# First loads of a two-layer decoder trunk cut into K tiles and interleaved, with constant products on TensorE at the start

## The chip, the cores and the metric

The kernel runs on one core of a Trainium2 chip. The metric is the device time of one execution in microseconds (us), the median over runs. One launch computes the whole reference.

## The reference

Two decoder layers over 256 positions of width 2048, all in float32. What matters here is the start of layer 0:

```python
def _rmsnorm(x, g):
    x32 = x.astype(jnp.float32)
    y = x32 * lax.rsqrt(jnp.mean(x32 * x32, axis=-1, keepdims=True) + EPS)
    return (y * g.astype(jnp.float32)).astype(x.dtype)

for l in range(DEPTH):                       # DEPTH = 2
    h = _rmsnorm(x, attn_norm_g[l])          # x: (1, 256, 2048)
    proj = h @ w_in[l]                       # w_in[l]: (2048, 6144)
    q, k, v, gate_b, gate_c, conv_in = jnp.split(proj, splits, axis=-1)
    # differential attention on q, k, v; gated causal convolution on the rest
    ...
    x = x + jnp.concatenate([attn, conv], axis=-1) @ w_out[l]
    hm = _rmsnorm(x, mlp_norm_g[l]) @ w_up[l]
    x = x + jnp.square(jax.nn.relu(hm)) @ w_down[l]
```

## The kernel before

**Products in three terms.** Every large product runs on TensorE in the type float32r. To keep accuracy, both operands are split into a rounded part (`hi`, made by a ScalarE copy) and the remainder (`lo`, made by a VectorE subtraction), and three of the four products are summed: hi x hi, hi x lo, lo x hi (`TERMS`). So for each K tile (128 rows of the contraction) and each of the two tiles of 128 positions, `linear` issues three matmuls of 512 columns (line 338): six per K tile, and sixteen K tiles for one block of 512 output columns. The first block is the first half of q of layer 0.

**The activations.** x lies in four tiles `xs[n]` of 512 columns, each four K tiles. `Norm.chunk` (line 394) takes one: for each of two pairs j of K tiles it transposes them on TensorE into a PSUM bank (line 402), and evicts each with the gain multiplied in, as a rounded part on ScalarE (line 248) and a remainder on VectorE (line 249). Then it squares the two position tiles of x on ScalarE for the norm's sum (line 412). The row factors of the norm are applied after the product, so matmuls need not wait for them. `Parts.ready` says that a chunk is there.

**The weights.** `Weights` holds a list of jobs. A job loads 512 KB (two K tiles by 512 columns) on SyncE's DMA queue (line 298), and `halves` splits it into `hi` (line 282) and `lo` (line 283). In layer 0 the first two jobs are split in two pieces, one K tile each. `take` makes jobs up to three ahead of the one that is used. Loads use four buffers, and `hi` and `lo` three each. `load_early` issues loads ahead of their jobs: `first_loads` (line 986) alternates two weight loads and one chunk of x.

**The order of the work.** TensorE's instructions run in the order in which the program is written. For the other engines and the DMA queues a scheduler, at build time, chooses the order by its own model of the times, with the order written as the priority; on the chip each engine then executes that fixed order. `late` (line 118) ties an instruction behind the one that was written just ahead of it on the same engine. `Background` holds generators that are advanced by ticks: `linear` ticks once after each K tile, and in a loop while it waits for a chunk of x. So the wait numbers decide behind which K tile a chunk's transposes stand: chunk 0 in front of K tile 0, chunk 1 behind K tile 1, chunk 2 behind K tile 5.

Of the kernel before, what the change touches and what calls it, by code (L numbers as in the profile page):

```python
# [15 lines left out]
P = 128  # L16
# [85 lines left out]
def trunk(ctx: ExitStack, tc: tile.TileContext, x, w_in, w_out, conv_w, q_norm_g, k_norm_g,  # L102
# [19 lines left out]
    def bank(name):  # L122
        return ps.tile([P, CH], F32, tag="bank", name=name)
# [8 lines left out]

    def load_x(n, cuts=1):
        for c in range(cuts):
            lo, hi = c * CH // cuts, (c + 1) * CH // cuts
            nc.sync.dma_start(
                xs[n][:, :, lo:hi],
                x[0, :, n * CH + lo:n * CH + hi].rearrange("(t p) c -> p t c", p=P))

    NG = DEPTH * D // P  # L140
    ngv = const.tile([NG, P], F32, tag="ngv", name="ngv")
    nc.scalar.dma_start(ngv, attn_norm_g.rearrange("l (k p) -> (l k) p", p=P))
    load_x(0, 2)

    ident = const.tile([P, P], F32, tag="ident", name="ident")
    make_identity(nc, ident)
    mhalf = const.tile([P, NH], F32, tag="mhalf", name="mhalf")
    nc.vector.memset(mhalf, -0.5)


# [29 lines left out]
    nc.gpsimd.dma_start(rel[0:NB, :], rel_bias)  # L180
    ones = const.tile([P, P], F32, tag="ones", name="ones")
    nc.vector.memset(ones, 1.0)

# [68 lines left out]
    class Parts:  # L252


        def __init__(self, pool, tag, name):
            self.make = lambda: pool.tile([P, 2, KG, S], F32R, tag=tag, name=name)
            self.ap = None
            self.ready = False

# [5 lines left out]
    class Weights:  # L265
# [8 lines left out]
        def halves(self, raw, c=slice(None)):  # L274

            i = len(self.made)
            shape = [P] + list(raw.shape[1:])
            hi = wpool.tile(shape, F32R, tag="hi", name="whi")
            lo = wpool.tile(shape, F32R, tag="lo", name="wlo")
            first = self.cut and i < 2  # L280
            for k in (slice(0, 1), slice(1, None)) if first else (slice(None),):
                nc.scalar.activation(hi[:, k], raw[:, k], AF.Copy)  # L282
                nc.vector.tensor_sub(lo[:, k], raw[:, k], hi[:, k].bitcast(F32))  # L283
            return hi, lo
# [3 lines left out]
        def plain(self, w, row, c, nk):  # L288

            cols = 2 * CH // nk  # L290

            def make():
                raw = self.early.pop(0) if self.early else load()
                return self.halves(raw)

            def load():
                raw = self.pool.tile([P, nk, cols], F32, tag="raw", name="raw", bufs=RAW)
                nc.sync.dma_start(
                    raw, w[row:row + nk * P, c:c + cols].rearrange("(k p) c -> p k c", p=P))
                return raw  # L300

            make.load = load
            self.jobs.append(make)
# [6 lines left out]
        def take(self):  # L310
            i = self.used
            self.used += 1
            while len(self.made) < min(len(self.jobs), i + 1 + AHEAD):
                self.made.append(self.jobs[len(self.made)]())
            return self.made[i]
# [9 lines left out]
    def linear(name, acts, weights):  # L325

        acc = mm.tile([P, NT, CH], F32, tag="mm2", name=name)
        nk = len(acts) * KG
        for kp in range(nk // 2):
            hi, lo = weights.take()  # L330
            for j in range(2):
                k = kp * 2 + j
                a = acts[k // KG]
                while not a.ready:
                    work.tick()
                for t in range(NT):
                    for n, (pa, pw) in enumerate(TERMS):
                        nc.tensor.matmul(  # L338
                            acc[:, t], a.ap[:, pa, k % KG, t * P:(t + 1) * P], (hi, lo)[pw][:, j],
                            start=(k == 0 and n == 0), stop=(k == nk - 1 and n == 2))  # L340
                work.tick()
        return acc

    def linear_t(name, acts, weights):
# [6 lines left out]
        for k0 in range(0, nk, 4):  # L351
            hi, lo = weights.take()
            a = acts[k0 // KG]
            while not a.ready:
                work.tick()
# [29 lines left out]
    class Norm:  # L385
# [8 lines left out]
        def chunk(self, n, wait):  # L394
            yield wait
            a = self.tiles[n].open()
            for j in range(2):
# [7 lines left out]
                for i in range(2):  # L405
                    k = 2 * j + i
                    split_gained(a, k, tp[:, i * S:(i + 1) * S],
                                 norm_gain(self.which, self.l, n * KG + k))
            self.tiles[n].ready = True
            for t in range(NT):  # L410
# [6 lines left out]
        def factors(self):  # L417
            while not all(t.ready for t in self.tiles):
                yield 1
# [66 lines left out]
    def attention(l, qT, kT, v, h0, dst, bias, tmp):  # L486
# [83 lines left out]
        yield from staggered([unit(t, i) for t in range(NT) for i in range(4)], 4)  # L570
        dst.ready = True

# [12 lines left out]
    def in_parts(dst, j, value):  # L585

        hi, lo = (dst.open()[:, i, 2 * j:2 * j + 2] for i in range(2))
        nc.scalar.activation(hi, value, AF.Copy)
        nc.vector.tensor_sub(lo, value, hi.bitcast(F32))
        dst.ready = j == 1  # L590

# [75 lines left out]
    def mlp(l, mnorm, last):  # L667
# [3 lines left out]
        with ExitStack() as scope:  # L671
# [127 lines left out]
            def up_part(acc, kh):  # L799
# [4 lines left out]
                for part, wt in ((0, hi), (1, lo)):  # L804
                    for k in range(8):
                        a = mT[kh * 2 + k // KG]
                        while not a.ready:
                            work.tick()
# [177 lines left out]
    def first_loads(weights):  # L986
        for n in range(1, D // CH):
            weights.load_early(2)
            load_x(n)
            work.start(norm.chunk(n, 2), 4 * n - 3)  # L990

    work.start(norm.chunk(0, 0))
    for l in range(DEPTH):
# [33 lines left out]
```

## Time and profile before

| | |
|---|---|
| median of 3 runs | 2178.97 us (2178.82 to 2180.45) |
| profiled execution, its own time | 2181.14 us |
| its span in the profile | 2179.4 us |
| TensorE busy | 2156.6 us, 99% |
| VectorE busy | 1603.9 us, 74% |
| ScalarE busy | 1271.7 us, 58% |

The profile comes from one execution, whose own time is a little above the median. In its rows the engines are PE (TensorE matmuls), PEld (its weight loads), DVE (VectorE), ACT (ScalarE), POOL (GpSimd) and SP (SyncE). A row of a timeline gives start, duration, engine, line, operation, the written and read tiles, and how many instructions of a kind are merged; in brackets, the idle time in front and what ended it. Successive instructions of an engine can overlap a little in their durations, so the distance from start to start is what one occupies. A row of the table by windows gives, for each engine, busy time and number of instructions, then the granted clock, the DMA share and GB/s. A row on DMA issues ends with the KB of one and the time from issue to landing.

### The profile page before, as it was taken

To read this page: it belongs to the slowest core of one execution; us is meant where nothing else is said; L and a number is where in the kernel's file an instruction comes from. 1 tells how busy PE (TensorE), PEld (TensorE's weight loads), DVE (VectorE), ACT (ScalarE), POOL (GpSimd) and SP (SyncE) were. 2 spreads that over 40 slices of the span, in tenths; PEclk is the share of its full clock that TensorE was granted. 3 is DMA by queue.
4 is the path that set the end of the run, shared out by engine and by line. 5 is a ranking of instruction groups with operands and counts; after the bars stand their busy time and mean duration, and the time that the engine had idled before them with its cause. 6 is when DMAs were issued, how large, how long until landed. Compare 5 with 4: busy or idle time off the path is not lost.

```text
span 2179.4 us, 29050 instructions
## 1 busy us (share of the span) xinstructions
PE 2156.6 (99%) x11066; PEld 1828.6 (84%) x11066; DVE 1603.9 (74%) x2229; ACT 1271.7 (58%) x1718; POOL 138.8 (6%) x194
## 2 busy tenths in 40 slices
PE   8999999999999999999999999999999999999999
PEld 6888888888888888888888888888888888888887
DVE  6677655698888888855566776557988888887554
ACT  6456445566666666654454654455666666665443
POOL 2021100000000000100011111000000000001000
PEclk9999999999999999999999999999999999999999
DMA  7555656476666666587565466656766666666774
GB/s 256 180 156 177 218 185 184 157 238 223 213 212 215 220 208 214 189 277 241 175 205 181 156 199 197 184 173 190 225 218 217 213 212 216 219 208 212 246 242 145
DMA packets 292491, 446.62 MB, mean 205 GB/s; under 512 B 10403, under 2 KB 191221, under 8 KB 292352
## 3 DMA queue, kind: packets, MB, share of 16 engines
q1 hardware_dynamic: 285648, 423.66, 61.5%
q0 software_dynamic: 6656, 21.10, 2.6%
q8 instruction: 86, 1.41, 0.3%
q14 instruction: 53, 0.43, 0.1%
q10 hardware_dynamic: 48, 0.02, 0.0%
HBM read 425.84 MB, written 18.90 MB: 204 GB/s over the span
## 4 chain that ended last, share of the span: by engine, by line
PE 94%; DMA 2%; DVE 2%; ACT 1%; issue 1%; SPq 0%; DVEq 0%; ACTq 0%
PE upc L809 29%; PE dn L969 15%; PE pr L849 13%; PE o L338 8%; PE q L338 4%; PE gc L360 4%; PE ci L360 4%; PE k L338 4%; PE gb L360 4%; PE v L338 4%; PE upw L809 1%; DMA uraw<-in_w_up_dram 1%; PE sc L500 1%; PE av L536 1%; PE tpn L402 1%; DMA draw<-in_w_down_dram 1%
## 5 line engine op out<-in xcount | busy, mean ns | idle before, releaser
L283 DVE TENSOR_TENSOR wlo<-raw,whi 128x1024 fp32r<-128x1024 f32 (+1 forms) x386 | 473.3, 1228 | 385.5 <-ACT whi L282 381.0
L282 ACT ACTIVATE whi<-raw 128x1024 fp32r<-128x1024 f32 (+1 forms) x386 | 406.8, 1055 | 477.8 <-PE dn L969 166.7
L809 PE MATMUL upc<-nT,uhi 128*128 128x512 f32 x1920 | 477.5, 391 | 0.0
L694 ACT ACTIVATE uhi<-uraw 128x1024 fp32r<-128x1024 f32 x256 | 271.2, 1060 | 287.3 <-PE upc L809 253.9
L809 PEld LDWEIGHTS upc<-nT,uhi 128*128 128x128 f32 x1920 | 352.7, 188 | 68.2
L695 DVE TENSOR_TENSOR ulo<-uraw,uhi 128x1024 fp32r<-128x1024 f32 x256 | 312.8, 1222 | 115.3 <-ACT uhi L694 112.9
L969 PE MATMUL dn<-whi,g 128*128 128x512 f32 x1024 | 316.4, 389 | 0.0
L809 PEld LDWEIGHTS upc<-nT,ulo 128*128 128x128 f32 x1920 | 261.9, 190 | 18.7
L809 PE MATMUL upc<-nT,ulo 128*128 128x256 f32 x1920 | 267.7, 282 | 0.0
L969 PEld LDWEIGHTS dn<-whi,g 128*128 128x128 f32 x1024 | 192.2, 188 | 39.7
L969 PE MATMUL dn<-wlo,g 128*128 128x512 f32 x512 | 199.6, 390 | 1.1 <-DVE wlo L283 1.0
L338 PE MATMUL o<-whi,cat 128*128 128x512 f32 x512 | 159.6, 390 | 0.0
L969 PEld LDWEIGHTS dn<-wlo,g 128*128 128x128 f32 x512 | 96.1, 188 | 22.6 <-DVE wlo L283 2.8
L338 PEld LDWEIGHTS o<-whi,cat 128*128 128x128 f32 x512 | 96.2, 188 | 19.7
L338 PE MATMUL o<-wlo,cat 128*128 128x512 f32 x256 | 99.6, 389 | 0.0
L831 POOL DMA_DIRECT2D hid<-h x64 | 34.9, 545 | 949.1 <-ACT h L830 913.4
L849 PE MATMUL pr<-t13h,f 128*128 128x512 f32 x240 | 93.8, 391 | 0.0
L338 PE MATMUL q<-whi,nT 128*128 128x512 f32 x256 | 86.4, 406 | 4.1 <-ACT nT L248 4.1
L338 PE MATMUL k<-whi,nT 128*128 128x512 f32 x256 | 85.3, 399 | 0.0
L849 PE MATMUL pr<-t24h,f 128*128 128x512 f32 x240 | 84.0, 391 | 0.0
L849 PE MATMUL pr<-b2h,f 128*128 128x512 f32 x240 | 84.0, 391 | 0.0
L338 PE MATMUL v<-whi,nT 128*128 128x512 f32 x256 | 83.4, 396 | 0.0
(330 smaller groups left out, 3431.0 us busy)
## 6 DMA issues: line engine op xcount, KB each, us to landing
uraw<-in_w_up_dram SPq DMA_DIRECT2D x128, 1024.0 KB, 5.9
raw<-in_w_in_dram SPq DMA_DIRECT2D x192, 512.0 KB, 3.9
draw<-in_w_down_dram SPq DMA_DIRECT2D x64, 1024.0 KB, 5.1
raw<-in_w_down_dram SPq DMA_DIRECT2D x64, 1024.0 KB, 5.7
raw<-in_w_out_dram SPq DMA_DIRECT2D x64, 512.0 KB, 3.6
hid<-h POOLq DMA_DIRECT2D x64, 256.0 KB, 4.3
back<-hid SPq DMA_DIRECT2D x32, 512.0 KB, 3.3
rev<-by_dist_d POOLq DMA_DIRECT2D x4, 1024.0 KB, 11.1
```

Source lines behind the costliest of these rows:

```text
L282: nc.scalar.activation(hi[:, k], raw[:, k], AF.Copy)
L283: nc.vector.tensor_sub(lo[:, k], raw[:, k], hi[:, k].bitcast(F32))
L338: nc.tensor.matmul(acc[:, t], a.ap[:, pa, k % KG, t * P:(t + 1) * P], (hi, lo)[pw][:, j], start=(k == 0 and n == 0), stop=(k == nk - 1 and ...
L360: nc.tensor.matmul(acc[:, f, 0] if part else acc[:, f], wt[:, k % 4, fs], a.ap[:, 0, k % KG] if part else a.ap[:, :, k % KG], start=(part ...
L402: nc.tensor.transpose(tp[:, i * S + t * P:i * S + (t + 1) * P], xs[n][:, t, k * P:(k + 1) * P], ident)
L500: nc.tensor.matmul(sc[:, :W], qT[m * DK:(m + 1) * DK, a, i, t * P:(t + 1) * P], kT[m * DK:(m + 1) * DK, b, i, :W], start=(n == 0), stop=(n ...
L694: nc.scalar.activation(hi, src, AF.Copy)
L695: nc.vector.tensor_sub(lo, src, hi.bitcast(F32))
L809: nc.tensor.matmul(acc[:, 0] if part else acc, wt[:, k], a.ap[:, 0, k % KG] if part else a.ap[:, :, k % KG], start=(part == 0 and kh == 0 ...
L831: nc.gpsimd.dma_start(hid[i // 2][:, i % 2 * 2 * S:(i % 2 + 1) * 2 * S], u)
L849: nc.tensor.matmul(prods[n], fs[j][:, pa, a], b[pw], start=(j == 0 and m == 0), stop=(stop and m == 2))
L969: nc.tensor.matmul(acc[:, t], f[:, pa, k, t * P:(t + 1) * P], (hi, lo)[pw][:, k % 2], start=(b == 0 and k == 0 and m == 0), stop=(b == NB2 ...
```

## The change

- x's first chunk and the first weight load are cut in two each and issued in turn: half of the chunk's columns, the first K tile of the weights, the other half, the second K tile. Before, both halves of the chunk went first and the weights followed in one DMA.
- `ones` is written at the start, and five products of it with itself (128 x 128 x 128, float32, into a PSUM bank of their own) stand ahead of the first TensorE work, and five more behind the transposes of K tiles 0 and 1.
- The first chunk yields between its two pairs: K tiles 0 and 1 are transposed and evicted before anything of the first weights is written, and K tiles 2 and 3 follow behind K tile 0's matmuls. `ready` becomes a count of K tiles.
- The first two jobs' roundings are tied by `late`, and `take` looks ahead by 0, 0, 1, 2 and then 3 jobs in layer 0.
- The chunks 1 to 3 start one K tile later than before (their transposes stand behind K tiles 2, 6 and 10).

```diff
-    def load_x(n, cuts=1):
-        for c in range(cuts):
-            lo, hi = c * CH // cuts, (c + 1) * CH // cuts
-            nc.sync.dma_start(
-                xs[n][:, :, lo:hi],
-                x[0, :, n * CH + lo:n * CH + hi].rearrange("(t p) c -> p t c", p=P))
+    def load_x(n, lo=0, hi=CH):
+        nc.sync.dma_start(
+            xs[n][:, :, lo:hi],
+            x[0, :, n * CH + lo:n * CH + hi].rearrange("(t p) c -> p t c", p=P))
...
-    load_x(0, 2)
+
+    ones = const.tile([P, P], F32, tag="ones", name="ones")
+    nc.vector.memset(ones, 1.0)
+    warm = bank("warm")
+
+    def warm_up(n):
+
+        for _ in range(n):
+            nc.tensor.matmul(warm[:, :P], ones, ones, start=True, stop=True)
...
+    warm_up(5)
...
             for k in (slice(0, 1), slice(1, None)) if first else (slice(None),):
-                nc.scalar.activation(hi[:, k], raw[:, k], AF.Copy)
-                nc.vector.tensor_sub(lo[:, k], raw[:, k], hi[:, k].bitcast(F32))
+                a = nc.scalar.activation(hi[:, k], raw[:, k], AF.Copy)
+                d = nc.vector.tensor_sub(lo[:, k], raw[:, k], hi[:, k].bitcast(F32))
+                if first:
+                    late(a)
+                    late(d)
...
-                nc.sync.dma_start(
-                    raw, w[row:row + nk * P, c:c + cols].rearrange("(k p) c -> p k c", p=P))
+                src = w[row:row + nk * P, c:c + cols].rearrange("(k p) c -> p k c", p=P)
+                if self.cut and not self.made and not self.early:
+                    for k in range(nk):
+                        load_x(0, k * CH // 2, (k + 1) * CH // 2)
+                        nc.sync.dma_start(raw[:, k], src[:, k])
+                else:
+                    nc.sync.dma_start(raw, src)
...
-            while len(self.made) < min(len(self.jobs), i + 1 + AHEAD):
+            ahead = min(max(i - 1, 0), AHEAD) if self.cut else AHEAD
+            while len(self.made) < min(len(self.jobs), i + 1 + ahead):
...
-                while not a.ready:
+                while a.ready <= k % KG:
                     work.tick()
...
-            self.tiles[n].ready = True
+                self.tiles[n].ready = 2 * j + 2
+                if j == 0 and n == 0 and (self.which, self.l) == (0, 0):
+                    yield 1
...
             load_x(n)
-            work.start(norm.chunk(n, 2), 4 * n - 3)
-
-    work.start(norm.chunk(0, 0))
+            work.start(norm.chunk(n, 2), 4 * n - 2)
+        work.start(norm.chunk(0, 0))
+        work.tick()
+        warm_up(5)
+
```

The other places that set or read `ready` (attention, convolution, the transposed products, the MLP) are only rewritten for the count.

More of the change, by code (lines that the diff above doesn't have):

```diff
@@ L180, in trunk @@
     nc.gpsimd.dma_start(rel[0:NB, :], rel_bias)
-    ones = const.tile([P, P], F32, tag="ones", name="ones")
-    nc.vector.memset(ones, 1.0)
     gains = const.tile([P, ROWS], F32, tag="gains", name="gains")
@@ L257, in __init__ @@
             self.ap = None
-            self.ready = False
+            self.ready = 0
         def open(self):
@@ L353, in linear_t @@
             a = acts[k0 // KG]
-            while not a.ready:
+            while a.ready < KG:
                 work.tick()
@@ L417, in factors @@
         def factors(self):
-            while not all(t.ready for t in self.tiles):
+            while not all(t.ready == KG for t in self.tiles):
                 yield 1
@@ L570, in attention @@
         yield from staggered([unit(t, i) for t in range(NT) for i in range(4)], 4)
-        dst.ready = True
+        dst.ready = KG
     def conv(l, q, u, cv, norm):
@@ L589, in in_parts @@
         nc.vector.tensor_sub(lo, value, hi.bitcast(F32))
-        dst.ready = j == 1
+        dst.ready = KG * j
     def gate(q, acc, cv, dst):
@@ L806, in up_part @@
                         a = mT[kh * 2 + k // KG]
-                        while not a.ready:
+                        while a.ready <= k % KG:
                             work.tick()
```

## The prediction

> **What bounds the kernel now.** I read the page first, then the chain that ended last over the first 30 us, then each engine's timeline there, then the DMA issues one by one.
>
> ```profile
> span 2179.4 us, 29050 instructions
> ...
> PE 2156.6 (99%) x11066; PEld 1828.6 (84%) x11066; DVE 1603.9 (74%) x2229; ACT 1271.7 (58%) x1718; POOL 138.8 (6%) x194
> ```
>
> TensorE (PE) is busy for 2156.6 of 2179.4 us, so 22.8 us of idle time is all that a better overlap can remove. The change adds work to PE and touches only the start. The chain there:
>
> ```profile
> 1.72 6.60 DMA raw<-in_w_in_dram
> ...
> 8.88 0.61 ACT whi L282
> 9.49 0.37 ACT nT L248
> ...
> 9.90 5.49 PE q L338 x12
> 15.39 1.15 PE tpn L402 x8
> 16.54 5.49 PE q L338 x24
> 22.03 0.87 PE tpn L402 x8
> ```
>
> The first matmul starts at 9.90. It waits for the first weight load (call the 512 KB loads w0, w1, ...), its rounding, and the eviction of the first transposes. Twelve matmuls (K tiles 0 and 1) then take 5.49 us, 0.46 each; the next 24 (K tiles 2 to 5) take the same 5.49, 0.23 each. So the PE runs at half pace until about 15.4, though the column for the granted clock, behind the busy times here, reads 1.00 in both stretches:
>
> ```profile
> 9.90:15.40 5.50, 5.50 (x14) 4.08 (x14) 4.39 (x8) 4.24 (x10) 1.05 (x2) 1.00 1.06 383
> 15.40:20.90 5.50, 5.50 (x28) 4.71 (x28) 3.62 (x8) 4.46 (x10) 0.00 (x0) 1.00 0.94 320
> ```
>
> I use a landmark: K tile 4, the first of the second chunk of x, starts half-way through the 24, at 16.54 + 2.75 = 19.29, and ends six matmuls later, at 20.66. Behind it the chain is PE alone, so what K tile 4 gains, the end gains, if later supply holds.
>
> ```profile
> 3.50 0.31 PE L152 MATMUL gps<-ident,ngv 32*128 32x32 f32 x1 [3.50 <-POOL ident masks.py:199]
> 3.81 2.01 PE L402 MATMUL tpn<-ident,x 128*128 128x128 f32 x8
> 9.90 0.80 PE L338 MATMUL q<-whi,nT 128*128 128x512 f32 x1 [4.09 <-ACT nT L248]
> ...
> 8.34 1.15 ACT L282 ACTIVATE whi<-raw 128x512 fp32r<-128x512 f32 x2 [5.85 <-DMA raw<-in_w_in_dram]
> 9.40 0.82 ACT L248 ACTIVATE nT<-tpn,ngains 128x256 fp32r<-128x256 f32 x2
> 10.11 1.14 ACT L282 ACTIVATE whi<-raw 128x512 fp32r<-128x512 f32 x2
> 11.15 0.83 ACT L248 ACTIVATE nT<-tpn,ngains 128x256 fp32r<-128x256 f32 x2
> 11.86 0.64 ACT L412 ACTIVATE junk<-x 128x512 f32<-128x512 f32 x1
> 13.08 1.06 ACT L282 ACTIVATE whi<-raw 128x1024 fp32r<-128x1024 f32 x1
> ...
> 1.04 0.17 DVE L182 MEMSET ones<- 128x128 f32 x1
> 9.00 1.29 DVE L283 TENSOR_TENSOR wlo<-raw,whi 128x512 fp32r<-128x512 f32 x2 [4.96 <-ACT whi L282]
> 10.21 0.87 DVE L249 SCALAR_TENSOR_TENSOR nT<-tpn,ngains,nT 128x256 fp32r<-128x256 f32 x2
> 14.18 1.23 DVE L283 TENSOR_TENSOR wlo<-raw,whi 128x1024 fp32r<-128x1024 f32 x1 [1.11 <-ACT whi L282]
> ```
>
> The transposes of chunk 0 begin at 3.81 and are done by 5.82, but ScalarE (ACT) evicts them only at 9.40, behind the rounding for which it idled 5.85 us. From starts in these rows: a rounded half tile takes ACT 0.53 us (8.34 to 9.40 for two), an evicted transpose 0.36 (9.40 to 10.11), the two squares 1.22 (11.86 to 13.08). On VectorE (DVE) half a rounding takes about 0.6 and an eviction 0.4.
>
> **The change, part by part.** The DMAs. SP issues, and the time from issue to landing of each:
>
> ```profile
> 0.72 0.95 SPq L136 DMA_DIRECT2D x<-in_x_dram  x2
> 1.72 0.46 SPq L298 DMA_DIRECT2D raw<-in_w_in_dram  x1
> 2.23 0.47 SPq L298 DMA_DIRECT2D raw<-in_w_in_dram  x1
> 2.74 0.47 SPq L136 DMA_DIRECT2D x<-in_x_dram  x1
> 3.25 0.51 SPq L298 DMA_DIRECT2D raw<-in_w_in_dram  x1
> 3.80 0.84 SPq L298 DMA_DIRECT2D raw<-in_w_in_dram  x1
> ...
> x<-in_x_dram SPq DMA_DIRECT2D x1, 256.0 KB, 3.0
> x<-in_x_dram SPq DMA_DIRECT2D x1, 256.0 KB, 3.4
> raw<-in_w_in_dram SPq DMA_DIRECT2D x1, 512.0 KB, 6.6
> raw<-in_w_in_dram SPq DMA_DIRECT2D x1, 512.0 KB, 7.4
> x<-in_x_dram SPq DMA_DIRECT2D x1, 512.0 KB, 8.4
> raw<-in_w_in_dram SPq DMA_DIRECT2D x1, 512.0 KB, 9.1
> raw<-in_w_in_dram SPq DMA_DIRECT2D x1, 512.0 KB, 10.0
> ```
>
> In order of issue, the first half of x lands at 3.7, the second at 4.6, w0 at 8.3, w1 at 9.6, the second chunk of x at 11.1, w2 at 12.35, w3 at 13.8. The change issues half x, half w0, half x, half w0. The first x half stays at 3.7. The first half of w0 is second in the queue: bounds 4.6 (what landed there) and 8.3; I take about 5.5, since the second place is the nearer row. The last half of w0 has the same bytes ahead of it as w0 had: 8.3, at best 6.5. There is one issue more, so w1 and all behind it are issued 0.5 us later; behind 8.3 the landings are 1.2 to 1.5 apart, a busy queue, so I put that at nothing, at most 0.5.
>
> The first warm-up. Five products of 128 columns. The nearest row is the product of `rbc`, 256 columns in fp32:
>
> ```profile
> 37.64 0.43 PE rbc L444 x2
> ```
>
> Half the columns is 0.21 each at full pace, 0.43 at half pace: 5 x 0.43 = 2.15, from about 1.0 (`ones` is written near there today, at 1.04, and becomes DVE's first instruction) to 3.2. PE starts on the transpose of the gains, `gps`, at 3.5 today, so they cost nothing.
>
> K tile 0. Its transposes end at 3.81 + 4 x 0.25 = 4.8 at the latest. ACT evicts two tiles (4.8 to 5.5), then rounds the first half of w0 (5.5 to 6.1); DVE has the low part at 6.75. The second five products run from 4.8 to 6.9 at half pace, 5.9 at full: up to the moment at which the operands are there, so 0 to 0.2. K tile 0 runs from 6.9: 6 x 0.23 to 8.25, or 6 x 0.46 to 9.65. Then four transposes (half of 0.87 or twice that).
>
> K tile 1 needs the last half of w0: landed 8.3, rounded 8.9, low part 9.6, so it ends at about 10.8.
>
> K tile 2 is where the change takes some back. The rounding of w1 is tied behind the instruction traced ahead of it on ACT, and that is now the second square of chunk 0; the squares are tied behind the eviction of K tile 3. So ACT runs last half of w0 (to 8.85), two evictions (to 9.55), two squares (to 10.8), w1's first half (to 11.35); DVE's part is ready at 12.0. Today w1 is rounded ahead of the squares. K tile 2 runs 11.4 to 13.2, waiting 0.6 before and 0.4 in it. Then the eight transposes of chunk 1 (0.87, one K tile later than today) to 14.1, K tile 3 to 15.4. K tile 4 wants the low part of w2 (landed 12.35, +1.06, +1.23 = 14.7: there) and its own evicted low part, which DVE may do only after w3 (w3 high 14.65, low 15.9, eviction 16.35): 0 to 0.6 us of wait. So K tile 4 ends between 16.8 and 17.35 instead of at 20.66: **3.3 to 3.9 us** gained if PE is at full pace by 7.
>
> If PE is at half pace up to about 10.6, K tile 0 ends at 9.65, the transposes at 10.5, the squares at 12.4, w1's low part at 13.65; K tile 4 starts at about 16.95 instead of 19.29: 2.3 us. I take 3.2, since ten products and the transposes keep PE almost without a gap from 1.0 on, where today it stood idle from 5.8 to 9.9, and full pace came 5.5 us after work became dense.
>
> [...]
>
> Supply later: w4 is issued when the last low part of w0 is done (10.3 today, 9.6 then), w5 when w1's is, near 12.6; with the longest landing above, 10.0, it is there at 22.6, and K tile 10 needs it only near 25: no new stall, so nothing. Renaming `ready` to a count alters no other order, and the waits of the background work shift by one K tile. Their matmuls are the same.
>
> Sum: 2181.14 (the profiled execution, 1.74 over its span) - 3.2 = 2177.9; that execution lies 2.2 above the median shown, so the median becomes 2178.97 - 3.2 = **2175.8**. About 0.2% (4.4 us) is what a measurement of this kernel can tell from no change, and 3.2 lies inside it.
>
> **The rivals.**
> B, the clock stays at half pace to 15.4 as today, the products releasing nothing: K tile 2 ends at 15.7, K tile 4 starts at 17.9, 1.4 gained: 2177.6. For it: full pace has followed only dense matmuls here. Against: fp32 products fill the PE like any other.
>
> C, slower. ACT is in order, and its order is fixed at build time from modelled landings; today that order made it idle 5.85 us for w0 with ready evictions behind. If w2's rounding, which has no tie, is put ahead of the evictions of K tiles 2 and 3, ACT waits for w2 (12.35): w2 to 13.4, evictions 14.1, squares 15.3, w1 15.9 and 16.5; K tile 2 runs to 17.7, K tile 4 starts at 19.9: 0.6 lost, 2179.6. PE then idles from 10.8 to 15.9, longer than the 4.09 us after which it ran at half pace today; another 2.75 makes it 2182.3, and stalls of later chunks come on top. It decides where w2 is modelled to land before PE is through with K tile 0. Against: today's order has w2 behind the squares.
>
> D, more. The squares do not hold w1: w1 is rounded at 9.6, K tile 2 ends at 12.2, K tile 4 at 16.3: 4.4 gained, 2174.6. Against: the ties.
>
> E, the rebuilt schedule moves ACT and DVE work elsewhere. PE's later waits are
>
> ```profile
> PE up L809 <- ACT ev L819: 3.2, 2, 2.0
> PE pr L849 <- DVE f L841: 3.2, 4, 1.0
> ```
>
> Doubled, they cost 6.4 us on top of the sum, 2182.2; gone, 2169.4. Nothing in the change points there.
>
> **How the numbers follow.** Forecast 0.56, of which 0.10 falls beyond 0.2% through small shifts elsewhere; B 0.10; C 0.12, of which 0.08 goes past 0.2% with the clock down and later stalls; D 0.11; E 0.11 (0.04 faster, 0.06 slower, 0.01 same). Faster: 0.10 + 0.11 + 0.04 = 0.25. Slower: 0.08 + 0.06 = 0.14. Same: 0.46 + 0.10 + 0.04 + 0.01 = 0.61. The range runs from D less 1 us, 2173.5, to C without the clock's part, 2180.0, rounded up to 2180.3; C's rest and E lie outside, under 0.2.
>
> **What would show it.** Right: the first L338 matmul at 6.2 to 7; the six of K tile 0 partly at 0.46; two evictions ahead of the first rounding on ACT; two squares directly ahead of w1's rounding and a PE wait of 0.5 to 1.5 us at K tile 2; K tile 4 starting at 15.4 to 17. Wrong: w2's rounding ahead of the second two evictions, a PE gap over 3 us behind K tile 1, 0.46 us matmuls past 12, or new PE waits behind 20 us.

## The result and the profile after

The changed kernel takes 2183.91 us (median of 11, 2183.06 to 2187.08), the kernel before on the same chip 2179.15 (11, 2177.57 to 2181.89). The ratio is 1.0021 with a 95% interval of 1.0012 to 1.0030: 4.8 us slower, where 3.2 us faster was forecast, and 3.6 us above the range. Timed again beside the kernel before, the ratio was 1.0024 (1.0015 to 1.0033).

The first stretch of TensorE's timeline after (columns as before: start, busy time, engine, line, operation, count, and in brackets the idle time ahead and what ended it):

```profile
1.04 2.50 PE L149 MATMUL warm<-ones 128*128 128x128 f32 x10 [1.04 <-DVE ones L143]
...
5.11 2.34 PE L149 MATMUL warm<-ones 128*128 128x128 f32 x10
7.55 0.80 PE L354 MATMUL q<-whi,nT 128*128 128x512 f32 x1
...
9.73 0.42 PE L354 MATMUL q<-wlo,nT 128*128 128x512 f32 x1
...
14.15 0.50 PE L354 MATMUL q<-whi,nT 128*128 128x512 f32 x1 [1.94 <-ACT whi L289]
...
18.16 0.63 PE L354 MATMUL q<-whi,nT 128*128 128x512 f32 x2
```

The first matmul stands at 7.55 (9.90 before), half pace ends near 9.7, K tile 2 waits 1.94 us for the rounding of w1 (the second weight load), and K tile 4, the second of the two matmuls in the last row, starts at 18.4 where 15.4 to 17 was forecast. ScalarE's timeline over the same time says why; the first row is the table load of the kernel before, the others are after:

```profile
1.21 1.28 ACT L282 ACT_TABLE_LOAD   x1 [1.21 <-PEq L1012]
...
4.19 1.28 ACT L254 ACT_TABLE_LOAD   x1 [4.19 <-DVE ngains L162]
5.48 0.47 ACT L254 ACTIVATE nT<-tpn,ngains 128x256 fp32r<-128x256 f32 x1
6.51 0.47 ACT L254 ACTIVATE nT<-tpn,ngains 128x256 fp32r<-128x256 f32 x1 [0.55 <-DVE nT L255]
6.88 1.14 ACT L289 ACTIVATE whi<-raw 128x512 fp32r<-128x512 f32 x2
10.86 0.47 ACT L254 ACTIVATE nT<-tpn,ngains 128x256 fp32r<-128x256 f32 x1 [2.84 <-PE tpn L418]
...
12.26 0.62 ACT L430 ACTIVATE junk<-x 128x512 f32<-128x512 f32 x1
...
13.48 3.03 ACT L289 ACTIVATE whi<-raw 128x512 fp32r<-128x512 f32 x4
```

ScalarE's first operation is now an eviction that waits for the gains, and the table load waits with it: 4.19 to 5.47, uncovered. The two evictions of a pair start 1.03 us apart, each behind VectorE's of the one before, not 0.36. The squares (12.26 to 13.48) stand ahead of w1's rounding, as forecast. TensorE's longer waits behind the start that the first profile of before does not have, and a row of a second profile of before (e5):

```profile
PE q00tp L496 <- DVE q00n L487: 1.2, 1, 1.2
PE pr L867 <- ACT f L858: 0.6, 1, 0.6
PE rbc L462 <- DVE s_gain L216: 0.4, 1, 0.4
...
PE q00tp L478 <- DVE q00n L469: 0.8, 1, 0.8
```

They are at the second transposes of q (53 us), in the first layer's MLP (465 us, `f` holds the activations for its down products) and at the row factors, which `rbc` spreads over the partitions (39 us). The last row shows that 0.8 of the 1.2 at q can come in the kernel before too. Starts of work on TensorE in five profiles (e5, e6 and e9 below are the two kernels unchanged; `dn` is the last stage of the MLP):

| us | before | e5, before | after | e6, after | e9, after |
|---|---|---|---|---|---|
| first q matmul | 9.90 | 8.44 | 7.55 | 7.49 | 7.77 |
| first k matmul | 39.31 | 37.37 | 39.38 | 38.71 | 41.66 |
| second transposes of q | 52.04 | 51.02 | 53.63 | 52.86 | 54.61 |
| first dn matmul, layer 1 | 918.74 | 918.71 | 920.83 | 920.66 | 924.03 |
| last matmul | 2174.10 | 2173.92 | 2176.26 | 2174.57 | 2180.52 |
| time of the execution | 2181.14 | 2180.97 | 2183.91 | 2181.90 | 2187.86 |

By the means of these columns, over two profiles and three, the kernel after is 1.6 us late at the first k, another 0.6 at the second transposes of q, another 0.9 at the first dn, and nothing more to the end: 3.1 in all. The medians differ by 4.8 and 5.5; both profiles of before were longer than the median of their comparison, and 1.7 to 2.4 us are in none of the profiles.

### The profile page after: what moved, and what is told of

Read it like the earlier page. It is cut to its first block, busy times and chain, and to the rows that moved or that the text cites. A ratio compares the mean times of both kernels' runs of the same rounds, so it can differ in the third digit from the quotient of the medians.

```text
span 2182.1 us, 29092 instructions
## 1 busy us (share of the span) xinstructions
PE 2160.6 (99%) x11086; PEld 1831.2 (84%) x11086; DVE 1604.6 (74%) x2229; ACT 1271.9 (58%) x1718; POOL 140.6 (6%) x194
## 4 chain that ended last, share of the span: by engine, by line
PE 92%; DMA 3%; DVE 2%; issue 2%; ACT 1%; POOL 0%; DVEq 0%; ACTq 0%; POOLq 0%
PE upc L827 29%; PE dn L987 15%; PE pr L867 12%; PE o L354 8%; PE gc L376 4%; PE ci L376 4%; PE gb L376 4%; PE v L354 4%; PE k L354 4%; PE q L354 3%; DMA uraw<-in_w_up_dram 1%; PE upw L827 1%; PE sc L518 1%; PE av L554 1%; DMA back<-hid 1%
```

## The experiments

Each kernel was timed 11 times if no other count is given (e5 and e6 once, e9 10, e13 5), beside the kernel before on the same chip.

**The same kernels again.** e5 is the kernel before, e6 and e9 the kernel after, all unchanged.

> The kernel before, unchanged, profiled once more. If its first profile was a slow draw of the first weight load (theory 1), w0 lands near 6.3 us here as it did in the shifted kernel before, the first q matmul starts near 7.9 instead of 9.90, K tile 4 starts at 16.5 to 17.5 instead of 19.29 and the span is 2176.5 to 2178. Rival: the landing at 8.3 is what this kernel does, and the shifted kernel was the lucky draw: first matmul 9.9, K tile 4 at 19.3, span about 2179.4.

> The kernel after, unchanged, profiled once more. Theory 1: its start is set by ScalarE's table load and the evictions that alternate with VectorE, and not by a landing, so the first q matmul stands at 7.5 and K tile 4 near 18.4 within 0.5 us, and the later losses (a wait of about 0.4 at the product of the row factors, about 1.2 at the second transposes of q) come again; span 2181 to 2183. Rival: the start varies with the landings as before's does, and the first matmul moves by a microsecond or more.

> The kernel after, unchanged, timed beside the kernel before on the chip of the next three runs. The profiles account for 0.7 to 2.3 us (last matmul of the two profiles of after against the two of before: +2.16, +0.47, +2.34, +0.65). If they hold the whole cause, the ratio is 1.0003 to 1.0012; if the first comparison's 4.8 us is the size, it is 1.0015 to 1.0025 and the profiles miss some 2 to 3 us that only unprofiled executions show.

ScalarE's first rounding in e5, and TensorE's first matmul behind it:

```profile
6.88 1.15 ACT L282 ACTIVATE whi<-raw 128x512 fp32r<-128x512 f32 x2 [4.39 <-DMA raw<-in_w_in_dram]
...
8.44 0.79 PE L338 MATMUL q<-whi,nT 128*128 128x512 f32 x1 [2.45 <-ACT nT L248]
```

w0 landed at 6.9 instead of 8.3, and K tile 4 started at 17.2 instead of 19.2. In the nine profiles whose first loads are those of before, w0 landed between 6.3 and 8.3, in the middle at 7.2. The first profile of before had the latest of them, so 1 to 2 us of what the change was to gain is not there in a usual execution. But e5 ended only 0.2 us sooner: of the 1.9 us that it was ahead at the first k, 0.9 went at the second transposes of q, and the rest in the MLP, where the clock fell. The rows are busy times in a stretch and, behind them, the granted clock, first of before, then of e5:

```profile
412.00:416.00 4.00, 3.68 (x20) 3.20 (x21) 1.75 (x3) 1.73 (x3) 0.00 (x0) 1.00 0.38 132
```

```profile
412.00:416.00 4.00, 4.00 (x16) 3.53 (x15) 0.68 (x2) 1.52 (x2) 0.00 (x0) 0.59 0.19 67
```

There TensorE waits 0.5 and then 1.9 us between the first up products, in both. The clock is under 1.00 behind that in 5 of 19 profiles (e5, e8, e11, e14, e15), and at the same place of layer 2 in two (e1, e14); each time it costs 1.7 us (4 us times the missing share, summed: in e5 4 x 0.41, and 4 x 0.01 in the next 4 us; at half pace that is 3.4 us, as in e9's rows from about 16.5 to 19.9), in the others nothing. e9, the kernel after, loses it in two other places:

```profile
16.00:20.00 4.00, 4.00 (x15) 3.41 (x16) 3.82 (x7) 2.34 (x5) 0.00 (x0) 0.57 0.55 162
464.00:468.00 4.00, 2.75 (x16) 2.22 (x14) 1.62 (x2) 2.54 (x4) 0.00 (x0) 1.00 1.01 315
468.00:472.00 4.00, 3.25 (x10) 2.33 (x11) 4.00 (x6) 3.30 (x4) 0.00 (x0) 0.81 0.50 190
```

Its half pace lasted to about 13, the wait for w1's rounding (1.33) was followed by half pace from about 16.5 to 19.9, K tile 4 started at 21.0, and the MLP's waits of 1.28 and 0.72 brought it again.

Every execution's mean granted clock is on record, rounded to a thousandth of the span (2.2 us), so means over many executions can be compared where there is no profile. In e9's comparison eight of the ten executions of after are under 1.000, three of them at 0.998; of the 32 of before eight are at 0.999 and none is lower. As lost time that is 2.4 us against 0.5, and 1.9 of the 5.4 us between the two means. The eleven executions of after in the result come to 2.2. But beside the other experiments the kernel before comes to 1.2 to 1.5, so the kernel after loses 0.7 to 1.9 us more of the clock. This is an estimate: it includes half pace behind the last matmul, where it costs nothing, in both kernels (up to 1.7 us; in before from about 2176.5). Why the kernel after loses more is not shown; in e9 half pace followed waits of 1.33 us at K tile 2 and 1.28 in the MLP, which the first profile of before does not have.

e6's expectation, a start within 0.5 us, failed: the first matmul repeats, K tile 4 stood at 17.7, 18.4 and 21.0.

Full pace came at about 6, 9.7 and 13 us in three executions of one kernel (e6, after and e9; in e6 ten records of the second products took 1.67 us, after 2.34), so here its moment was not tied to the kernel's start. Half pace followed idle stretches of 1.3 us in e9, and of 0.5 and 1.9 with 3.7 us of matmuls between in e5.

**The later order alone.** e1 and e17 are the kernel before with chunks 1 to 3 and the bias table one K tile later; e2 is the kernel after with the bias table one tick back.

```
-            work.start(load_bias(l, bpool, bias), 10)
+            work.start(load_bias(l, bpool, bias), 10 + (l == 0))      # e1, e17; e2: 10 - (l == 0)
-            work.start(norm.chunk(n, 2), 4 * n - 3)
+            work.start(norm.chunk(n, 2), 4 * n - 2)                   # e1, e17
```

> The kernel before with one thing of the change: the background work of layer 0 (chunks 1 to 3, the bias table, the row factors) one K tile later. Theory A (the time lost behind 30 us comes from this shift: the bias table's small product stands one K tile later, its two DMAs and what is queued behind them on POOL and ACT slide into the normalisation of q): 1.2 to 2.3 us over before, about 2180.4 to 2181.4, with PE waits at the product of rbc (about 0.4) and at the transposes of q (about 1.2). Rival B (the loss comes from the new order of loads and roundings at the start): within 0.5 us of before, no such waits.

> The kernel before with the statistics of chunks 1 to 3 and the bias table one K tile later, once more (0.9995 the first time, the one version under 1). If its lower profile was a draw of the first weight load and of the clock alone: 0.9997 to 1.0003 and a profile that differs from its first by 1 us or more at the first q matmul or in the MLP. If the later bias table is worth something by itself: 0.9992 to 0.9997.

> The changed kernel with the bias table's setup started at tick 9 instead of 10, so that its product stands behind K tile 8 again. Theory A: the wait at the transposes of q (1.2 us, about 1.5 with the refill) goes; the one at rbc may stay, since the row factors still stand one K tile later; 2181.8 to 2182.7 against 2183.9. Rival B: no change, 2183.9.

e1 came to 0.9995 (0.9986 to 1.0004), e17 to 0.9997 (0.9989 to 1.0006), with no wait at the row factors: the shift by one K tile costs nothing by itself. e2 came to 1.0008 (0.9999 to 1.0017). Its interval overlaps that of after, so by the times alone the tick may be worth nothing, but its profile shows what it moves. `by_dist` and `rev` are two steps of the bias table, which goes through DRAM, and `row_e` is the first operation of the row factors. GpSimd's timeline after, then in e2:

```profile
30.27 0.49 POOL L208 DMA_DIRECT2D by_dist_d<-by_dist  x1 [19.25 <-DVE by_dist L207]
34.09 1.85 POOL L241 DMA_DIRECT2D rev<-by_dist_d  x2 [3.34 <-DMA by_dist_d<-by_dist]
36.02 0.19 POOL L396 TENSOR_SCALAR row_e<-tot 128x2 f32<-128x2 f32 x1
```

```profile
29.52 1.84 POOL L241 DMA_DIRECT2D rev<-by_dist_d  x2 [1.53 <-DMA by_dist_d<-by_dist]
33.72 0.19 POOL L396 TENSOR_SCALAR row_e<-tot 128x2 f32<-128x2 f32 x1 [2.36 <-DVE tot L439]
```

After, the row factors' first operation starts the moment the two issues of rev are done: it stood behind them in GpSimd's queue, and they behind by_dist's way through DRAM, whose copy stood behind a weight's low part on VectorE. In e2 GpSimd waits for its operand alone, and the 0.4 at rbc is gone. The second wait, at q's transposes, was still 0.6.

**The start.** e3 gives the four transposed tiles of chunk 0 a bank each; e4 leaves out the products; e7 adds products (five and four) to the kernel before; e8 removes from the kernel after four causes together; e16 is e8 without its products.

```
+    tab = const.tile([P, 1], F32, tag="tab", name="tab")              # e8, e16
+    nc.scalar.activation(tab, ones[:, 0:1], AF.Copy)
...
+                tps = [tp, bank(f"tpm{n}_{j}") if own else tp]        # e3, e8, e16
...
+            if n == 0 and (self.which, self.l) == (0, 0):             # e8, e16: squares behind w1
+                yield 2
...
-            work.start(norm.chunk(n, 2), 4 * n - 2)
+            work.start(norm.chunk(n, 2), 4 * n - 2 - (n > 1))         # e8, e16; bias table as in e2
...
-    warm_up(5)                                                        # e4, e16, in both places
```

> The changed kernel with the four transposed K tiles of chunk 0 in PSUM banks of their own. Theory A (the two evictions of a pair alternate with VectorE because both engines read one bank, 1.03 us for each instead of 0.36): the first rounding starts about 0.6 us earlier, the squares another 0.7, K tile 4 starts about 1.2 us earlier than the 18.4 of the changed kernel, and the end follows by 0.8 to 1.2. Rival B (they alternate because ScalarE and VectorE would anyhow, the weights decide): K tile 4 within 0.3 us.

> The changed kernel without the ten constant products. Theory A (they bring full pace forward): the first matmul still near 7.2 to 7.6, but half pace lasts about 5.5 us from there, to near 13, and K tile 4 starts 0.5 to 1.5 us later than 18.4; the end 0.5 to 1.5 later, about 2185. Rival B (the products do nothing, the pace follows the dense matmuls alone and the waits for weights decide): K tile 4 and the end as in the changed kernel.

> The kernel before with only the products on TensorE: five at the front and four behind the first chunk's transposes, with ones made earlier for them. If the products bring full pace forward by themselves, as in the kernel after against the one without them (about 4 us earlier), K tiles 0 and 1 run mostly at 0.23 us a matmul, K tile 4 starts 1 to 2.5 us sooner than in the kernel before with the same landing of w0, and the end comes 1 to 2.5 us sooner: ratio 0.999 to 0.9995. Rival: between the last product and the first matmul (about 7 to 8 or 9.9) TensorE is idle long enough to lose the pace again: half pace to about 12, no gain.

> The kernel after with its four suspected costs taken out together: one small operation of ScalarE at the front so that its table load is done before the first eviction; the four K tiles of the first chunk in banks of their own; the squares of the first chunk traced behind the rounding of w1; the bias table one tick sooner and the statistics of chunks 2 and 3 one K tile sooner. My theory (start terms plus two later waits) expects: first matmul 6.3 to 6.9, K tile 4 at 15.3 to 16.3, no waits at the product of the row factors and the second transposes of q, and a span 5 to 6 us under the kernel after's: 2176 to 2177, ratio 0.9975 to 0.999. Rival (a faster start only moves the wait to later loads or to ScalarE's rounding of w4 and w5): the gain at K tile 4 is given back by K tile 10, span 2179 or more, ratio 0.9995 to 1.001.

> The repaired kernel after (early table load, own banks, squares later, bias table and statistics sooner) without its products on TensorE: the candidate to beat both, with as many TensorE instructions ahead of the MLP as the kernel before. Theory: half pace to about 11 to 12 us, so 0.5 to 1.5 us later at the first k than the repaired kernel, but the packet of instructions is fetched 6 us or more behind the first down-weight load's issue, that load takes 7.5 to 7.8 us instead of 8.32, and the MLP gives nothing back: ratio 0.999 to 0.9997. Rival (the products' later cost is not their instructions): load 8.3 or more, ratio 1.0000 to 1.0008.

e3's ScalarE rows:

```profile
4.12 1.28 ACT L254 ACT_TABLE_LOAD   x1 [4.12 <-DVE ngains L162]
5.41 0.47 ACT L254 ACTIVATE nT<-tpn,ngains 128x256 fp32r<-128x256 f32 x1
5.78 0.47 ACT L254 ACTIVATE nT<-tpm,ngains 128x256 fp32r<-128x256 f32 x1
...
17.41 1.06 ACT L289 ACTIVATE whi<-raw 128x1024 fp32r<-128x1024 f32 x1 [2.01 <-DMA raw<-in_w_in_dram]
18.37 0.82 ACT L254 ACTIVATE nT<-tpn,ngains 128x256 fp32r<-128x256 f32 x2
```

Two banks bring the evictions back to 0.37 apart, and the first matmul to 6.82. K tile 4 starts at 16.1, more than the 1.2 us sooner that was expected, but full pace came at about 7.5 in this execution, so not all of it is the banks' work. The rebuilt order then put w4's rounding, which waited 2.01 for its landing, ahead of chunk 1's last two evictions; TensorE waited 1.23 and 0.56, its clock fell to 0.64, and the ratio was 1.0020 (1.0011 to 1.0029). That is the mechanism of the forecast's rival C, one chunk later. Without products (e4) half pace lasted to 14.5 and K tile 4 started at 19.4, so against this one profile the products bring full pace forward by 1.5 to 8.5 us; yet the ratio, 1.0013 (1.0004 to 1.0022), is no worse than with them. Products alone on the kernel before (e7) gave 1.0006 (0.9997 to 1.0015): no gain, though K tile 4 was at 16.3. With all four repairs (e8) the ratio is 1.0000 (0.9991 to 1.0009): the loss is gone, but there is no gain, against an expected 0.9975 to 0.999. Its table load and two of TensorE's waits:

```profile
1.21 1.28 ACT L146 ACT_TABLE_LOAD   x1 [1.21 <-PEq L1038]
...
PE q L356 <- DVE nlam L229: 0.6, 1, 0.6
PE q L356 <- DVE nT L257: 0.5, 1, 0.5
```

The first matmul stands at 7.14 and K tile 4 starts at 15.3, 1.9 us ahead of e5. The two waits, both for VectorE, stand behind K tile 4 (16.4 and 23.6), and the first k, at 37.14, is only 0.2 ahead of e5: the faster start was given back there, which is the rival that e8's expectation names. e16 came to 1.0012 (1.0003 to 1.0022), missing its expectation: K tile 4 starts at 16.1, and waits of 1.4 and 0.6 for chunk 1's evictions stand behind it, as in e3.

**The MLP.** e10 puts six products of 128 columns into the 1.9 us wait in each layer's MLP of the kernel before. e11 is e7 with the shift of e1, e12 both e11 and e10. e13 adds 24 products of two columns behind chunk 0's transposes of the kernel before; e14 and e15 add 12 (eight columns) and 10 (two columns) in the first layer's MLP to e8 and e2.

```
+                            if (kh, c) == (1, 1):                      # e10, e12; e14, e15 in layer 1
+                                for _ in range(6):
+                                    nc.tensor.matmul(fill[:, :P], ones, ones,
+                                                     start=True, stop=True)
                             up_part(two[c], kh)
```

> The kernel before, with six constant products on TensorE in the 1.9 us in which it waits between the first up products of each layer's MLP. Theory (the pace of TensorE at that place is a draw: half pace for 1.4 to 1.7 us in three of six profiles, after two idle stretches of 0.5 and 1.9 us): no clock under 1.00 at 404 to 420 and 1484 to 1500, and the time 0.5 to 1.5 us under before's, ratio 0.9993 to 0.9998. Rival (that loss is in the profiled executions alone, or the products delay what stands behind them): ratio 0.9999 to 1.0006.

> The kernel before, with five products at the front and four behind the first chunk's transposes, and with the statistics of chunks 1 to 3 and the bias table one K tile later, as they stand against the K tiles in the kernel after. Theory (the earlier start is worth its 2.9 us only if the row factors and the bias table do not come late): no wait at the second transposes of q, offset there -2.5 to -4.2 us against the first profile of before, span 2176 to 2177.5, ratio 0.9985 to 0.9995. Rival (the bias table's landing then sets the second transposes of q wherever the K tiles stand): wait of 0.8 to 1.1 us again, offset -1.5 to -2.5, ratio 0.9995 to 1.0005.

> The run before this one with the six products in each MLP's gap as well: the candidate to beat both. If start, row factors and the MLP's clock are the three places, the ratio is 0.998 to 0.999 (2176 to 2178); if one of the two halves of the argument is wrong, it falls together with that half's own run, 0.9993 to 1.0003.

> The kernel before, with 24 products of two columns behind the first chunk's transposes, in the gap in which TensorE idles: about 96 more TensorE instructions ahead of everything, and no other change that reaches the MLP. TensorE's instructions come by DMA in packets of 16 KB, one for 256 instructions, and each added instruction makes the next packet start some 0.1 us earlier against the work. Theory (the packet that falls into the flight of the first down-weight load of the first layer's MLP costs that load a microsecond): with 24 to 40 instructions more the packet starts 2.4 to 4.0 us after that load's issue and the load takes 8.3 to 9.6 us in ten profiles; with 96 it starts before the issue, so the load takes 7.5 to 7.8 us as in the kernel before, the wait of ScalarE for the next load (at 458 to 463) is under 4.2 us instead of 4.6 to 5.7, TensorE does not wait for its product's operands near 464 to 466, and the ratio is 0.999 to 1.0003. Rival (any added instruction on TensorE, or the bank it takes, slows this stage): load 8.3 us or more, ratio 1.0005 to 1.002.

> The repaired kernel after (early table load, own banks, squares later, bias table and statistics sooner), with 12 products of two columns in the gap between the first up products of the first layer's MLP: 88 TensorE instructions over the kernel before, where the repaired one has 40. ScalarE's, VectorE's and the queues' orders are the repaired one's. Theory: first down-weight load 7.5 to 7.8 us instead of 8.32, no clock under 1.00 at 404 to 420, 1 to 2 us gained over the repaired kernel: ratio 0.9985 to 0.9995 (2176.5 to 2179). Rival: as the repaired kernel, 0.9995 to 1.0005.

> The kernel after with the bias table one tick sooner, and 10 products of two columns in the first layer's MLP gap: 80 TensorE instructions over the kernel before instead of 40. Theory: first down-weight load 7.5 to 8 us instead of 8.53, TensorE's wait near 465 gone, 0.5 to 1.4 us gained over the kernel with the bias table alone (1.0008): ratio 1.0000 to 1.0006. Rival: 1.0006 to 1.0015.

e10 is the cleanest: the order of every other engine and queue is that of the kernel before, and it costs 1.0015 (1.0006 to 1.0024). e11 came to 1.0018 (1.0009 to 1.0027), e12 to 1.0014 (1.0005 to 1.0023). What they share with the kernel after is a later landing of `draw`, a 1 MB load of down weights in the first layer's MLP. (It is the third such load there; the expectations call it the first.) Its issue by SyncE and the ScalarE operation that waits for it, before, after, and in e13:

```profile
436.56 0.37 SPq L701 DMA_DIRECT2D draw<-in_w_down_dram  x1
...
444.25 0.63 ACT L714 ACTIVATE b1h<-draw 128x512 fp32r<-128x512 f32 x1 [1.51 <-DMA draw<-in_w_down_dram]
461.20 0.63 ACT L714 ACTIVATE b1h<-draw 128x512 fp32r<-128x512 f32 x1 [3.85 <-DMA draw<-in_w_down_dram]
```

```profile
432.14 1.84 SPq L705 DMA_DIRECT2D uraw<-in_w_up_dram  x2
437.43 0.37 SPq L719 DMA_DIRECT2D draw<-in_w_down_dram  x1
...
446.20 0.63 ACT L732 ACTIVATE b1h<-draw 128x512 fp32r<-128x512 f32 x1 [2.56 <-DMA draw<-in_w_down_dram]
463.32 0.63 ACT L732 ACTIVATE b1h<-draw 128x512 fp32r<-128x512 f32 x1 [5.03 <-DMA draw<-in_w_down_dram]
```

```profile
442.97 0.37 SPq L705 DMA_DIRECT2D draw<-in_w_down_dram  x1
...
450.54 0.63 ACT L718 ACTIVATE b1h<-draw 128x512 fp32r<-128x512 f32 x1 [1.62 <-DMA draw<-in_w_down_dram]
```

From issue to use it takes 7.69, 8.77 and 7.57 us. Everything behind shifts with it: the next `draw` is issued later, ScalarE, in order, waits 5.03 for it (3.85 before), and TensorE 0.6 for ScalarE's `f`. What the profiles show different on the way is one packet of a queue that carries instructions (q8). The page's row of that queue after, with TensorE's row (before: 86 packets, and 11066 of each):

```profile
PE 2160.6 (99%) x11086; PEld 1831.2 (84%) x11086; DVE 1604.6 (74%) x2229; ACT 1271.9 (58%) x1718; POOL 140.6 (6%) x194
...
q8 instruction: 87, 1.43, 0.3%
```

22172 instructions of TensorE over 87 packets are 255 in each, 16 KB (before, 22132 over 86 are 257), so I take q8 for TensorE's code. In the DMA view of 441.0 to 441.5 after, and of 443.0 to 443.5 before, stands one such packet:

```profile
q8 instruction: 1, 0.02, 11.1%
```

```profile
q8 instruction: 1, 0.02, 11.8%
```

11.1% of sixteen engines for 0.5 us is 0.9 us of one of them. After, it comes 3.6 us behind `draw`'s issue, in its flight; before, 6.4 us behind, when the load is nearly done. The change's ten products are 20 records of matmuls and 20 of weight loads (11086 against 11066 of each). These 40 instructions bring the packet forward. Over all 19 profiles, by when the packet comes against `draw`'s issue:

| packet (start of its half-microsecond), us against the issue | profiles | `draw`, issue to use, us | layer 1, first up to first dn, less the lost clock |
|---|---|---|---|
| 6.0 to 6.6 behind | before, e1, e4, e5, e16, e17 | 7.44 to 7.70 | 518.0 to 519.0 |
| 6.0 ahead | e13 | 7.57 | 518.1 |
| 5.5 ahead to 4.0 behind | after, e2, e3, e6 to e12, e14, e15 | 8.21 to 9.62 | 518.7 to 520.2 |

The two up-weight loads ahead of `draw` are issued 5.3 and 3.8 us before it and share its queue. e14's packet came up to 0.3 us behind the first of them, and `draw` took 8.51; e13's came 0.2 to 0.7 ahead of it, and `draw` took 7.57. The third row's mean in the last column is 519.5 (519.4 without the four that have products of their own there), that of the others 518.5: by these means the packet costs 1.0 us there, though the two ranges overlap a little and the kernels differ in more than the packet. e13 was expected to set `draw` free by moving the packet ahead, and did; e16 by taking the products out, and did (7.67). Their times say nothing on it, since e13 lost 5.7 us at the start to its own products (10.24 us for 24; 1.0038, 1.0024 to 1.0051) and e16 has the waits above. e14 (1.0002, 0.9993 to 1.0010) and e15 (1.0016, 1.0007 to 1.0025) moved the packet to other places in the flight, so they missed what was expected of them. e8 and e14 are equal to the kernel before although their `draw` is late too (8.32 and 8.51). e10 lost no clock in either MLP, but its 3.2 us are more than the packet's 1.0; neither its profile nor its clock on record (0.8 us lost, 0.5 before) shows a cause for the rest.

TensorE's waits in the profile after, 15.4 us in all, are put down to other engines and to one load of x, none to its own code; what shows is a weight load that lands later (8.77 us from issue to use, 7.69 before).

No version beat the kernel before: e1, e2, e7, e8, e14 and e17 are equal to it within their intervals.

## Why the prediction was wrong

Two steps failed that the sum rests on: ScalarE's time for the first two evictions, which with the pace set K tile 4 back to 18.4, and the other orders of work, whose cost was put at nothing. By the prediction's own steps:

- **K tile 4 at 19.29 as the point to gain from.** One execution (19.15 in its rows). w0's landing at 8.3, which the prediction quoted, was late: 6.9 in e5, and 6.3 in e1, whose first loads are those of before. The prediction saw that the profiled execution lay 2.2 us above the median, and took the whole 3.2 from the median all the same. 1 to 2 us of the gain were in that profile alone.
- **The first half of w0 near 5.5.** It landed at 4.9, inside the bounds. Right, but it was not what K tile 0 waited for.
- **"ACT evicts two tiles (4.8 to 5.5)".** This step failed. The table load, hidden before under the wait for w0, follows ScalarE's first operation and is uncovered (1.28). The price 0.36 was read from two tiles whose VectorE parts came later; with both engines on one bank in turn it is 1.03. The rounding started at 6.88 instead of 5.5, and the same 1.03 came again at K tiles 2 and 3. e3 shows the second part alone (0.37 apart with a bank each), and in e8 the table load is covered again, at 1.21.
- **Full pace by 7.** It came at 9.7, 6 and 13; the 10.6 of the 2.3 us case was the author's estimate, and no run shows it. The products did bring the pace forward (e4), but by an amount that differs between executions: the forecast and its 2.3 us case were both draws of one thing.
- **Squares ahead of w1, K tile 2 at 11.4.** The order was right. Its start was 14.15, since each term before it was late; the wait was 1.94, not 0.6, and in e9 the one of 1.33 there was followed by half pace, at 1.7 us.
- **w4, "no new stall".** Right after. But with K tile 4 at 15.3 to 16.1, as early as the forecast had it (e3, e8, e14, e16), 1.1 to 4.5 us were lost again by the first k, against the 20.2 us that the kernel before takes from one to the other. So "what K tile 4 gains, the end gains" did not hold in this order of work; e7, in the order of before, kept what it had (16.3, then 20.2).
- **"Alters no other order, and the waits of the background work shift by one K tile".** Mis-sized at nothing. The order did shift, and ScalarE's and VectorE's order behind the first 60 instructions is unchanged, so rival E did not come. But by_dist and rev met the row factors in GpSimd's queue: 0.4 at rbc, with e2's tick as the proof, and perhaps part of the 1.2 at q's transposes (0.6 in e2, but 0.8 in e5).
- **"Their matmuls are the same."** True, and the MLP's loss was outside every step: ten products, counted as free where they stand, bring a packet of code, 430 us on, into a load's flight, for 1.0 us by the means above.
- **The rivals.** B did not come: the products' records stand without a gap (ten in 2.50 us), half pace ended near 9.7, and half pace to about 14.5 is what e4 has, without them. In D the squares should not have held w1, and they did. C's mechanism came, but only in e3.

What is shown: repairing the start and the two background steps together (e8) removes the whole loss, and e14, which is e8 with narrow products in the MLP, repeats it. Which of the four repairs carries it is not separated: the banks (e3) and the bias table's tick (e2) were tried alone, the table load and the squares were not. What is only argued: how the 4.8 us divide. By the profiles it is 1.6 to the first k (0.9 of it by K tile 4, and 0.4 at rbc), 0.6 at q, 0.9 in the MLP; 1.7 to 2.4 us of the medians' difference show in no profile. The clock on record puts 0.7 to 1.9 us on lost clock, of which the profiles hold about 0.3, so most of the missing time can be that; the rest stays open. In the second layer's MLP `draw` took 7.00 to 8.77 with no such split by the packet; that stays open too.

## What to carry to other kernels

Before a gain is read off a start, profile the kernel twice: here one load landed up to 2 us sooner or later in the same kernel, more than half of what the edit was to gain. An operation moved to the head of an engine's queue took the engine's table load with it (4.19 instead of 1.21), and evictions that two engines made in turn from one bank went at 1.03 us, with a bank each at 0.37. Instructions that cost nothing where they stand cost elsewhere here: they moved a packet of code into the flight of a load that ScalarE, in order, waits for (8.77 us instead of 7.69), for 1.0 us by the means above. Look where the packet falls after a change of the count.

## Not expected of the hardware

- With a packet of TensorE's code among three 1 MB loads, the one that is waited for lands about 1 us later (8.21 to 9.62 instead of 7.44 to 7.70), as above.
- TensorE fell to half pace after waits of 1.33 and 1.28 us in e9 and of 0.5 and 1.9 in e5, at a cost of 1.7 us each, and not after one of 1.94 in the profile after, nor after the same 0.5 and 1.9 in the first profile of before.
- GpSimd's power of 128x8 takes 1.64 us when it starts 0.09 us ahead of a VectorE subtraction of two SBUF operands, and 2.61 when it starts 0.11 behind, 1.5 past VectorE's end. The kernel before has the short form in its first profile and the long one in e5; after:

```profile
49.87 1.23 DVE L290 TENSOR_TENSOR wlo<-raw,whi 128x1024 fp32r<-128x1024 f32 x1 [0.27 <-ACT whi L289]
...
49.98 2.61 POOL L398 TENSOR_TENSOR q_r<-q_e,mhalf 128x8 f32<-128x8 f32 x1
```

- A product of two or eight columns costs nearly what one of 128 costs: 10.24 us for 48 records of two columns in e13 at half pace (0.21), 2.74 for 24 of eight in e14 (0.11), 1.50 for 12 of 128 in e10 (0.13). In the MLP's gap the clock held with 128 columns (e10, e12) and fell with the narrow ones (e14 0.57, e15 0.82 at 412). Two executions each show no rule: with nothing in the gap it held in 12 of 15.
